# Two projections at a time, matmul by matmul: a two-layer macaron block in float32r on Trainium2

## The chip, the core and the metric

The kernel runs on one core of one Trainium2 chip. The metric is the device time of one execution in microseconds, as the median of several executions. One further execution was recorded by the hardware profiler; its rows are what the prediction reads. "PE" is TensorE's matmul pipe and "PEld" its weight loads, "DVE" is VectorE, "ACT" ScalarE, "POOL" GpSimd, "SP" the queue that issues all DMAs here.

## The reference, cut to what matters

```python
for l in range(2):                                            # x: 512 tokens x 1024
    h = 0.5 * swiglu(x, w_gate[l, 0], w_up[l, 0], w_down[l, 0])   # 1024 -> 2816 -> 1024
    x = layernorm(ALPHA * x + h, ...)
    u = x @ w_in[l]                                           # 1024 -> 1792
    u_conv, u_lru, q, k, v = split(u, [512, 1024, 1536, 1664])
    y = concat(conv_module(u_conv), recurrent(u_lru), sliding_window_attention(q, k, v))
    x = layernorm(ALPHA * x + y @ w_out[l], ...)
    h = 0.5 * swiglu(x, w_gate[l, 1], w_up[l, 1], w_down[l, 1])
    x = layernorm(ALPHA * x + h, ...)
```

`swiglu` is `(silu(x @ wg) * (x @ wu)) @ wd`. Everything is float32.

## The kernel before, in words

There are six phases: FFN, mixer, FFN for each of two layers (`phases`, line 749). The 512 tokens are the moving operand of the first products, held transposed: `xH` and `xL` are the high and low part of x as float32r, eight blocks of 128 features by 512 tokens each. A float32 product is made of three float32r products, low weights by `xH`, high weights by `xL`, high weights by `xH` (lines 312 to 314). `split` (line 116) makes the two parts of anything: a cast on ACT, then a subtraction on DVE.

**`proj`** (line 307) makes one output block: 128 columns of a weight matrix by all 512 tokens, accumulated in one PSUM bank over 8 blocks of features with three matmuls each, so 24 matmuls of 512 columns. The kernel before calls it for one bank at a time: in an FFN (line 359) first for the gate tile `pg`, then for the up tile `pu` (lines 386 and 387), 22 times per FFN; in the mixer (line 421) through `tile_of` (line 444), for one block of 128 of the 1792 input columns, when the program comes to need it. `proj_first` (line 295) makes the first four blocks of a phase in two halves of the tokens (256 columns each), because the last two token blocks of x are still being normalised: half 0 of block 0, the transposes of token block 2 (`to_xT(2)`), half 0 of blocks 1 and 2, `to_xT(3)`, half 0 of block 3, then half 1 of all four.

After the gate and up products `act` (line 370) applies Silu on ACT (line 372), multiplies on DVE (line 373) and splits. The down projection (`rowmm`, line 348) has the hidden units as stationary operand and 512 columns of weights as moving one; it cycles through eight banks, two per token block. The output projection of the mixer uses the same `rowmm` in `partial` (line 705) and `attn_out`.

In the mixer the order of the input blocks is `order` (line 436): recurrent input 4 and 5, keys 12, values 13, recurrent gate 6 and 7, queries 8, 9, 10, 11. `query(j)` (line 581) makes block 8+j and copies it out of its bank on ACT (line 582). Queries 0 and 1 are made ahead of attention; `query(2)` and `query(3)` stand in the attention loop:

```python
for u in range(U + 2):          # 8 units of 4 heads by 128 queries
    if u < U:
        scores(u)
    if u < 2:
        query(2 + u)
    ...
    if 0 <= u - 1 < U:
        transpose_p(u - 1)
```

`scores(u)` (line 642) issues four score matmuls on PE, then bias and row minimum on DVE (line 655), exponentials on ACT (line 662); `normalise` (line 667) scales by the reciprocal of the sum on ACT or DVE; `transpose_p` (line 679) turns the probabilities on PE, which ACT or DVE copies out (lines 689, 691), and `weighted` (line 694) multiplies by the values. One step runs on each of these for units u, u-1 and u-2 per turn of the loop.

The order of instructions on each engine is set by a scheduler that works from the order of the program and its own costs. Weights come through two buffers `raw` and 14 buffers of the pool `wpool` (seven pairs of high and low part); PSUM has eight banks, taken in turn by `bank()`. Some weight pairs lie in the pool `tpool` instead, whose tiles are 1030 floats wide and not 1024: the fourth pair of `wb` in the mixer's end (line 743) is one.

Of the kernel before, what the change touches and what calls it, by code (L numbers as in the profile page):

```python
# [22 lines left out]
KC = D // P  # L23
# [10 lines left out]
LOOK = 3  # L34
# [13 lines left out]
def tile_hymba(  # L48
# [38 lines left out]
    def nm(s):  # L87
        uid[0] += 1
        return f"{s}_{uid[0]}"

    def bank():
        return psum.tile([P, 512], F32, tag="ps", name=nm("ps"))
# [7 lines left out]
    def mm(o, a, b, start, stop):  # L100
        nc.tensor.matmul(o, a, b, start=start, stop=stop)  # L101
# [12 lines left out]
    xL = cpool.tile([P, KC, S], F32R, name="xL")  # L114

    def split(hi, lo, src):
        """src == hi + lo, both with the 12 significant bits of float32r."""
        nc.scalar.copy(hi, src)  # L118
        nc.vector.tensor_tensor(lo, src, hi.bitcast(F32), op=ALU.subtract)  # L119

    def to_xT(t):
        for hf in range(2):
            pt = bank()
            for c in range(4):
                k = hf * 4 + c
                nc.tensor.transpose(pt[:, c * P:(c + 1) * P], xs[:, t, k * P:(k + 1) * P], ident)  # L126
            sl = (slice(None), slice(hf * 4, hf * 4 + 4), slice(t * P, (t + 1) * P))
            split(xH[sl], xL[sl], pt.rearrange("p (c t) -> p c t", c=4))

# [1 line left out]
    chT = cpool.tile([P, 2, DEPTH * NCH], F32, name="chT")  # L131
    cpos = cpool.tile([P, 2, DEPTH], F32, name="cpos")
    cneg = cpool.tile([P, 2, DEPTH], F32, name="cneg")
# [65 lines left out]
    gates = {}  # L199
# [82 lines left out]
            norm_b(t, st, coef, last)  # L282

    class Start:
        """Weights of a phase's first products, loaded while the phase before ends."""

        def __init__(self, thunks):
            self.thunks = list(thunks)
# [2 lines left out]
        def load(self, n=1, pool=None):  # L291
            for _ in range(n):
                self.pairs.append(self.thunks.pop(0)(pool))

    def proj_first(items):
        def part(pb, w, lo, hi):
            proj([(pb, w)], ((lo, hi),))
        for n, (pb, w) in enumerate(items):
            if n == len(items) - 1:
                to_xT(3)  # L300
            part(pb, w, 0, 256)
            if n == 0:
                to_xT(2)
        for pb, w in items:
            part(pb, w, 256, 512)

    def proj(items, parts=((0, S),)):
        """items: (bank, weight pair); each part of the tokens is done for all of them in turn."""
        for lo, hi in parts:
            for pb, (wh, wl) in items:  # L310
                for k in range(KC):
                    mm(pb[:, lo:hi], wl[:, k, :], xH[:, k, lo:hi], k == 0, False)
                    mm(pb[:, lo:hi], wh[:, k, :], xL[:, k, lo:hi], False, False)
                    mm(pb[:, lo:hi], wh[:, k, :], xH[:, k, lo:hi], False, k == KC - 1)

    def fetch_raw(src):
# [18 lines left out]
    def load_cols(src, c, pool=None, raw=None):  # L335
        pair = load(cols(src, c), pool, raw)
        return [w.rearrange("p (k f) -> p k f", k=KC) for w in pair]
# [21 lines left out]
    def ffn(l, i, idx, start, nxt, last, hooks={}):  # L359
        wg, wu, wd = w_gate[l, i], w_up[l, i], w_down[l, i]  # L360
        for si, (f0, f1) in enumerate(SLABS):
            fin = si == len(SLABS) - 1
            hA = hpool.tile([P, 8, S], F32R, tag="hA", name=nm("hA"))
            hB = hpool.tile([P, 8, S], F32R, tag="hB", name=nm("hB"))
            hC = hpool.tile([P, HC], F32R, tag="hC", name=nm("hC"))[:, :6 * S].rearrange("p (a s) -> p a s", a=6)

            def hparts(n):
                return (hA[:, n, :], hB[:, n, :]) if n < 8 else (hC[:, n - 8, :], hC[:, n - 5, :])

            def act(f, pg, pu):  # L370
                sg = spool.tile([P, S], F32, tag="sg", bufs=2, name=nm("sg"))
                nc.scalar.activation(sg, pg, AF.Silu)  # L372
                nc.vector.tensor_tensor(sg, sg, pu, op=ALU.mult)  # L373
                split(*hparts(f - f0), sg)

            f = f0
            if f0 == 0:
                start.load(len(start.thunks))
                items = [(bank(), w) for w in start.pairs]
                proj_first(items)  # L380
                for j in range(2):
                    act(j, items[2 * j][0], items[2 * j + 1][0])
                f = 2
            while f < f1:
                pg, pu = bank(), bank()
                proj([(pg, load_cols(wg, f))])
                proj([(pu, load_cols(wu, f))])
                act(f, pg, pu)
                if f in hooks:
                    hooks[f]()  # L390
                f += 1
            ys = [[bank(), bank()] for _ in range(NT)]

            def hpair(f, t):
                return [h[:, t * P:(t + 1) * P] for h in hparts(f - f0)]

            flow = f1 - RESIDENT if fin else f1
            for f in range(f0, flow):
                w = load_rows(wd, f)
                for t in range(NT):  # L400
                    rowmm(ys[t], hpair(f, t), w, f == f0, f == f1 - 1)
            if not fin:
                for t in range(NT):
                    for hf, sl in enumerate(HS):
                        nc.vector.scalar_tensor_tensor(xs[:, t, sl], ys[t][hf], 0.5 / ALPHA, xs[:, t, sl],
                                                       op0=ALU.mult, op1=ALU.add)
                continue
            coef = ln_coef(idx)
            ws = [load_rows(wd, f) for f in range(flow, f1)]
            if nxt:  # L410
                nxt.load(3)
                nxt.load(1, tpool)

            def rows(t):
                for w, f in zip(ws, range(flow, f1)):
                    rowmm(ys[t], hpair(f, t), w, f == f0, f == f1 - 1)
                return ys[t]

            tail(rows, 0.5 / ALPHA, coef, last)

    def mixer(l, idx, start, nxt):
# [8 lines left out]
        wl = w_in[l]  # L430
# [5 lines left out]
        order = [4, 5, 12, 13, 6, 7, 8, 9, 10, 11]  # L436
        ahead = {}

        def fetch(n):
            for c in order[:n]:  # L440
                if c not in ahead:
                    ahead[c] = load_cols(wl, c)

        def tile_of(c):
            fetch(order.index(c) + LOOK)
            pb = bank()
            proj([(pb, ahead[c])])
            return pb

        # conv input and gate  # L450
        gate_in = [bank() for _ in range(4)]
        proj_first(list(zip(gate_in, start.pairs)))
        nc.gpsimd.memset(yc[:, :, 0:30], 0.0)
# [35 lines left out]
            if n == CONV_OUT_AT:  # L489
                conv_out(cv[0])  # L490

        # recurrent input
        xb = scratch()
        xbv = xb[:, :2 * (S + 3)].rearrange("p (c s) -> p c s", c=2)
        nc.gpsimd.memset(xbv[:, :, 0:3], 0.0)
# [8 lines left out]
                nc.vector.scalar_tensor_tensor(xc[:, c, :], xbv[:, c, k:k + S], ch(c, 34 + k), xc[:, c, :],  # L504
                                               op0=ALU.mult, op1=ALU.add)

        # keys and values
        pk = tile_of(12)
        for g in range(2):
            own = slice(64 * g, 64 * g + 64)  # L510
# [6 lines left out]
        nc.scalar.copy(vT[:, :S], pv)  # L517
        point()

        # recurrent gates  # L520
        rv = pair_of(wpool)
        iv = pair_of(wpool)
        qv = pair_of(wpool)
# [12 lines left out]
            for c in range(2):  # L536
                nc.scalar.activation(rv[:, c, :], nv[:, c, :], AF.Sqrt)

        # recurrent output gate
        gel = pair_of()  # L540
        for c in range(2):
            nc.scalar.activation(gel[:, c, :], tile_of(6 + c), AF.Gelu_apprx_tanh)
# [202 lines left out]
        nxt.load(4)  # L745
        tail(lambda b: partial(b, wb, (2, 3, 0, 1)), 1.0 / ALPHA, coef, False, lambda: attn_out(NT - 1, wo))

# [1 line left out]
    phases = []  # L749
    for l in range(DEPTH):  # L750
        phases += [(ffn, (l, 0, 3 * l), ffn_start(l, 0)), (mixer, (l, 3 * l + 1), mixer_start(l)),
# [1 line left out]
    with tc.manual_schedule():  # L753
        first = phases[0][2]
# [66 lines left out]
```

## Time and profile before

| what | value |
|---|---|
| median of 3 executions | 1845.03 us (1844.8, 1845.03, 1847.89) |
| profiled execution, first to last instruction (span) | 1850.2 us |
| its own device time | not listed apart from the span |
| PE busy | 1826.9 us (99%), 8530 matmul records |
| DVE / ACT / POOL busy | 828.8 us (45%) / 608.7 us (33%) / 35.1 us (2%) |
| DMA engines busy | 31.1%, 176.88 MB |
| chain that ended last | PE 92%, DVE 3%, ACT 2%, DMA 2% |

Matmul records are pipelined: one of 512 columns is listed with about 0.39 us, while the next one starts 0.23 us later. So PE's pace is read from starts, or from the number of records in a stretch, and not from the length of a record.

### The profile page before, as it was taken

The page shows a single profiled execution, that of the slowest core. Times are in us where ns is not written, and L with a number is a line of the kernel's source. Part 1 is how long each engine was busy: PE and PEld are TensorE (multiplying, and loading weights), DVE is VectorE, ACT ScalarE, POOL GpSimd, SP SyncE. Part 2 cuts the span into 40 slices and gives each one's busy share as a digit, 9 for nine tenths or more (in the row PEclk, how much of TensorE's full clock was granted, in tenths as well). Part 3 has the DMA queues.
Part 4 walks back from the last instruction along what each step waited for, and adds up shares of the span by engine and source line. Part 5 has one row for each costly group of instructions (what it writes and reads, how often), then busy time and mean ns, then how long its engine had stood idle before and what let it go on. Part 6 is the DMA issues. An engine that isn't in the chain of part 4 may idle for free.

```text
span 1850.2 us, 20960 instructions
## 1 busy us (share of the span) xinstructions
PE 1826.9 (99%) x8530; PEld 1490.9 (81%) x8530; DVE 828.8 (45%) x1281; ACT 608.7 (33%) x912; POOL 35.1 (2%) x76
## 2 busy tenths in 40 slices
PE   8999999999999999999999999999999999999998
PEld 7788888898678888888898888888976888888886
DVE  4342333269875332433363323333889833233324
ACT  4222222233954221222233212222458432222221
POOL 1000000000000000000000000000000100000000
PEclk9899999999999999999999999999999999999999
DMA  6433333222133323333333233323212332233321
GB/s 182 143 114 102 91 96 97 92 81 63 60 111 118 91 91 103 91 92 98 107 103 92 92 99 95 91 93 101 83 48 69 119 109 92 93 101 91 93 89 46
DMA packets 234248, 176.88 MB, mean 96 GB/s; under 512 B 6963, under 2 KB 217000, under 8 KB 234152
## 3 DMA queue, kind: packets, MB, share of 16 engines
q1 hardware_dynamic: 234152, 175.54, 31.1%
q8 instruction: 67, 1.10, 0.2%
q14 instruction: 29, 0.24, 0.0%
HBM read 171.33 MB, written 3.67 MB: 95 GB/s over the span
## 4 chain that ended last, share of the span: by engine, by line
PE 92%; DVE 3%; ACT 2%; DMA 2%; issue 0%; SPq 0%; POOL 0%; DVEq 0%; POOLq 0%; ACTq 0%
PE ps L101 91%; ACT t L662 1%; PE ps L126 1%; DVE wl L119 1%; DMA raw<-in_ffn_w_up_dram 1%; DMA raw<-in_ffn_w_gate_dram 1%; DMA xs<-in_x_dram 0%; ACT wh L118 0%; ACT t L675 0%; DMA raw<-in_w_out_dram 0%; DVE t L655 0%; DVE t L569 0%; DVE yL L119 0%; DVE t L254 0%; ACT junk L259 0%
## 5 line engine op out<-in xcount | busy, mean ns | idle before, releaser
L101 PE MATMUL ps<-xH,wl 128*128 128x512 f32 (+1 forms) x1824 | 683.9, 375 | 0.3 <-DVE wl L119 0.3
L101 PE MATMUL ps<-xL,wh 128*128 128x512 f32 (+1 forms) x1824 | 680.7, 373 | 1.0 <-DVE xL L119 1.0
L101 PE MATMUL ps<-xH,wh 128*128 128x512 f32 (+1 forms) x1824 | 680.4, 373 | 0.0
L119 DVE TENSOR_TENSOR wl<-raw,wh 128x1024 fp32r<-128x1024 f32 x308 | 376.1, 1223 | 630.2 <-ACT wh L118 629.5
L118 ACT CAST wh<-raw 128x1024 fp32r<-128x1024 f32 x308 | 323.3, 1052 | 1012.2 <-PE ps L101 953.3
L101 PEld LDWEIGHTS ps<-xH,wl 128*128 128x128 f32 x1824 | 345.2, 189 | 69.1 <-DVE t L236 1.1
L101 PEld LDWEIGHTS ps<-xL,wh 128*128 128x128 f32 x1824 | 345.3, 189 | 67.2 <-DVE xL L119 1.2
L101 PEld LDWEIGHTS ps<-xH,wh 128*128 128x128 f32 x1824 | 345.1, 189 | 66.2
L101 PE MATMUL ps<-wl,hA 128*128 128x512 f32 x512 | 199.4, 389 | 0.0
L101 PE MATMUL ps<-wh,hA 128*128 128x512 f32 x512 | 199.2, 389 | 0.0
L373 DVE TENSOR_TENSOR sg<-sg,ps 128x512 f32<-128x512 f32 x88 | 60.5, 687 | 306.0 <-PE ps L101 306.0
L101 PE MATMUL ps<-wh,hB 128*128 128x512 f32 x512 | 158.3, 390 | 0.0
L101 PE MATMUL ps<-wh,hC 128*128 128x512 f32 x384 | 121.5, 389 | 0.0
L101 PEld LDWEIGHTS ps<-wl,hA 128*128 128x128 f32 x512 | 96.1, 188 | 20.1
L101 PEld LDWEIGHTS ps<-wh,hA 128*128 128x128 f32 x512 | 96.1, 188 | 19.9
L101 PEld LDWEIGHTS ps<-wh,hB 128*128 128x128 f32 x512 | 95.7, 188 | 19.6
L101 PEld LDWEIGHTS ps<-wh,hC 128*128 128x128 f32 x384 | 72.1, 188 | 15.0
L463 DVE SCALAR_TENSOR_TENSOR t<-mix,chT,t 128x512 f32<-128x512 f32 x120 | 81.7, 742 | 0.2
L101 PE MATMUL ps<-wl,hC 128*128 128x512 f32 x192 | 74.7, 389 | 0.0
L372 ACT ACTIVATE sg<-ps 128x512 f32<-128x512 f32 x88 | 52.0, 591 | 4.3 <-PE ps L101 4.3
L259 ACT ACTIVATE junk<-t,nmean 128x1024 bf16<-128x1024 f32 x24 | 27.7, 1153 | 77.2 <-DVE nmean L257 77.2
L101 PE MATMUL ps<-wl,yH 128*128 128x512 f32 x128 | 50.7, 396 | 0.0
(134 smaller groups left out, 1015.9 us busy)
## 6 DMA issues: line engine op xcount, KB each, us to landing
raw<-in_ffn_w_gate_dram SPq DMA_DIRECT2D x88, 512.0 KB
raw<-in_ffn_w_up_dram SPq DMA_DIRECT2D x88, 512.0 KB
raw<-in_ffn_w_down_dram SPq DMA_DIRECT2D x88, 512.0 KB
raw<-in_w_in_dram SPq DMA_DIRECT2D x28, 512.0 KB
raw<-in_w_out_dram SPq DMA_DIRECT2D x16, 512.0 KB
t<-in_ln_g_dram SPq DMA_DIRECT2D x6, 512.0 KB
t<-in_ln_b_dram SPq DMA_DIRECT2D x6, 512.0 KB
xs<-in_x_dram SPq DMA_DIRECT2D x4, 512.0 KB
```

The source lines that it names most:

```text
L101: nc.tensor.matmul(o, a, b, start=start, stop=stop)
L118: nc.scalar.copy(hi, src)
L119: nc.vector.tensor_tensor(lo, src, hi.bitcast(F32), op=ALU.subtract)
L126: nc.tensor.transpose(pt[:, c * P:(c + 1) * P], xs[:, t, k * P:(k + 1) * P], ident)
L259: nc.scalar.activation(junk, z[:, :D], AF.Square, bias=nmean, accum_out=rs)
L372: nc.scalar.activation(sg, pg, AF.Silu)
L373: nc.vector.tensor_tensor(sg, sg, pu, op=ALU.mult)
L463: nc.vector.scalar_tensor_tensor(ca[:, c, :], yc[:, c, k:k + S], ch(c, k), ca[:, c, :], op0=ALU.mult, op1=ALU.add)
L662: nc.scalar.activation(s4[:, h, :nk], s4[:, h, :nk], AF.Exp, bias=nm_[:, h:h + 1], scale=-1.0, accum_out=sm[:, h:h + 1])
```

## The change

`proj` gets two items at a time and goes through them inside the loop over feature blocks: for each of the three kinds of product the matmul into the first bank is followed by the same one into the second. The gate and up tile of an FFN are such a pair, and so are blocks 0 and 1, and 2 and 3, of `proj_first`. In the mixer `tile_of` makes the block asked for and the next one of `order` together, so the pairs are 4 and 5, 12 and 13, 6 and 7, 8 and 9, 10 and 11. The rest of the diff drops comments.

```diff
     def proj_first(items):
-        def part(pb, w, lo, hi):
-            proj([(pb, w)], ((lo, hi),))
-        for n, (pb, w) in enumerate(items):
-            if n == len(items) - 1:
+        for n in range(0, len(items), 2):
+            if n == len(items) - 2:
                 to_xT(3)
-            part(pb, w, 0, 256)
+            proj(items[n:n + 2], ((0, 256),))
             if n == 0:
                 to_xT(2)
-        for pb, w in items:
-            part(pb, w, 256, 512)
+        for n in range(0, len(items), 2):
+            proj(items[n:n + 2], ((256, 512),))
...
         for lo, hi in parts:
-            for pb, (wh, wl) in items:
-                for k in range(KC):
+            for k in range(KC):
+                for pb, (wh, wl) in items:
                     mm(pb[:, lo:hi], wl[:, k, :], xH[:, k, lo:hi], k == 0, False)
+                for pb, (wh, wl) in items:
                     mm(pb[:, lo:hi], wh[:, k, :], xL[:, k, lo:hi], False, False)
+                for pb, (wh, wl) in items:
                     mm(pb[:, lo:hi], wh[:, k, :], xH[:, k, lo:hi], False, k == KC - 1)
...
                 pg, pu = bank(), bank()
-                proj([(pg, load_cols(wg, f))])
-                proj([(pu, load_cols(wu, f))])
+                proj([(pg, load_cols(wg, f)), (pu, load_cols(wu, f))])
                 act(f, pg, pu)
...
+        made = {}
+
         def tile_of(c):
-            fetch(order.index(c) + LOOK)
-            pb = bank()
-            proj([(pb, ahead[c])])
-            return pb
+            if c not in made:
+                n = order.index(c)
+                fetch(n + 1 + LOOK)
+                two = order[n:n + 2]
+                for d in two:
+                    made[d] = bank()
+                proj([(made[d], ahead[d]) for d in two])
+            return made[c]
```

Two places of the scheduled order matter below. The first is ACT in the first mixer, around the scores of units 0 and 1. `t_3126` and `t_3127` are the query tiles (first and second pair), so a copy into `t_3127` marks the end of a product of query block 10 or 11; `t_3216` is unit 0's score tile, `t_3287` (before) and `t_3312` (after) unit 1's; the wide casts are weights. From `tile_of` on, lines of the changed kernel stand five further down (582 is 587). Before:

```order
L664 ACTIVATE es_3228<-es_3228 128x4
L118 CAST wh_3431<-raw_3429 128x1024
L675 ACTIVATE t_3216<-t_3216,ri_3281 128x128
L582 ACTIVATE t_3127<-ps_3236 128x512
L675 ACTIVATE t_3216<-t_3216,ri_3281 128x128 x3
L118 CAST wh_3480<-raw_3478 128x1024
L662 ACTIVATE t_3287,sm_3301<-t_3287,nm_3288 128x256 x4
L664 ACTIVATE es_3299<-es_3299 128x4
L118 CAST wh_3542<-raw_3540 128x1024
L552 ACTIVATE tw_3048<-tw_3048,cneg 128x512
L554 ACTIVATE tw_3048<-tw_3048,half 128x512 x2
L582 ACTIVATE t_3127<-ps_3307 128x512
```

And now:

```order
L667 ACTIVATE t_3216,sm_3230<-t_3216,nm_3217 128x128 x4
L669 ACTIVATE es_3228<-es_3228 128x4
L118 CAST wh_3373<-raw_3371 128x1024
L680 ACTIVATE t_3216<-t_3216,ri_3306 128x128 x4
L118 CAST wh_3431<-raw_3429 128x1024
L557 ACTIVATE tw_3048<-tw_3048,cneg 128x512 x2
L587 ACTIVATE t_3127<-ps_3236 128x512
L587 ACTIVATE t_3127<-ps_3237 128x512
L559 ACTIVATE tw_3048<-tw_3048,half 128x512
L667 ACTIVATE t_3312,sm_3326<-t_3312,nm_3313 128x256 x4
L669 ACTIVATE es_3324<-es_3324 128x4
```

Unit 1's exponentials stood between the copies of query blocks 10 and 11, and now stand behind both. The weight cast that stood directly ahead of them is gone from that place, and one of the two steps at line 559 (554 before) stands there instead.

The second place is DVE at the same point; `t_3287`, `t_3312` and the casts are as above, `wl` is the low part of a weight tile. Before:

```order
L119 TENSOR_TENSOR wl_3432<-raw_3429,wh_3431 128x1024
L655 ISA t_3287,nm_3288<-ps_3289,nbias,nsink 128x256
...
L119 TENSOR_TENSOR wl_3481<-raw_3478,wh_3480 128x1024
L659 TENSOR_TENSOR es_3299<-nm_3288,sink 128x4
L670 TENSOR_TENSOR sm_3301<-sm_3301,es_3299 128x4
L672 RECIPROCAL ri_3345<-sm_3301 128x4
L677 TENSOR_SCALAR t_3287<-t_3287,ri_3345 128x256 x4
L119 TENSOR_TENSOR wl_3543<-raw_3540,wh_3542 128x1024
L556 SCALAR_TENSOR_TENSOR tw_3049<-tw_3049,tw_3048 128x512 x2
```

And now:

```order
L119 TENSOR_TENSOR wl_3374<-raw_3371,wh_3373 128x1024
L119 TENSOR_TENSOR wl_3432<-raw_3429,wh_3431 128x1024
L660 ISA t_3312,nm_3313<-ps_3314,nbias,nsink 128x256
...
L561 SCALAR_TENSOR_TENSOR tw_3049<-tw_3049,tw_3048 128x512
L664 TENSOR_TENSOR es_3324<-nm_3313,sink 128x4
L565 SCALAR_TENSOR_TENSOR tw_3048<-tw_3049,tw_3048 128x512
L660 ISA t_3351,nm_3352<-ps_3353,nbias,nsink 128x128
```

Two weight subtractions now stand ahead of unit 1's scores, and none directly behind them. On PE the products themselves alternate: of the matmuls of `proj` that directly follow another one, 5241 went into the same bank as the one before them, and 32 do now (all in the first pair of the first phase, where the scheduler lets the gate run ahead of the up weights).

## Rows read from the trace of the kernel before

**Rows 1.** The page's part 1 (busy) and part 4 (chain), whole execution.

```profile
PE 1826.9 (99%) x8530; PEld 1490.9 (81%) x8530; DVE 828.8 (45%) x1281; ACT 608.7 (33%) x912; POOL 35.1 (2%) x76
...
PE 92%; DVE 3%; ACT 2%; DMA 2%; issue 0%; SPq 0%; POOL 0%; DVEq 0%; POOLq 0%; ACTq 0%
```

**Rows 2.** Windows, line 101: down, then gate and up (us, records, clock, DMA).

```profile
160.00:200.00 40.00, 40.00 (x178) 1.00 0.34 102
240.00:300.00 60.00, 60.00 (x258) 1.00 0.32 93
```

**Rows 3.** Instruction groups by shape, whole execution: one of three kinds of product.

```profile
L101 PE MATMUL ps<-xH,wl 128*128 128x512 f32 x1440 | 574.0, 399 | 0.0
```

**Rows 4.** Timeline of PE (start, length): end of an up product, then down.

```profile
151.12 0.40 PE L101 MATMUL ps<-xL,wh 128*128 128x512 f32 x1
151.35 0.39 PE L101 MATMUL ps<-xH,wh 128*128 128x512 f32 x1
151.59 0.63 PE L101 MATMUL ps<-wh,hB 128*128 128x512 f32 x2
152.05 0.39 PE L101 MATMUL ps<-wl,hA 128*128 128x512 f32 x1
```

**Rows 5.** Timeline of PE, end of a block of the output projection.

```profile
545.72 0.62 PE L101 MATMUL ps<-wh,yL 128*128 128x512 f32 x2
...
547.08 0.63 PE L101 MATMUL ps<-wh,yL 128*128 128x512 f32 x2
...
548.25 0.40 PE L101 MATMUL ps<-wh,yH 128*128 128x512 f32 x1
```

**Rows 6.** Chain in order of time (start, us, what), first mixer.

```profile
464.99 12.01 PE ps L101 x54
...
477.01 0.60 ACT t L582
...
478.48 0.94 ACT wh L118
...
483.08 1.14 DVE wl L119
484.22 1.20 DVE tw L556 x2
...
486.51 0.61 DVE tw L560
...
493.72 1.13 PE ps L101 x2
```

**Rows 7.** The same view, second mixer.

```profile
1369.91 17.31 PE ps L101 x70
...
1403.96 1.13 PE ps L101 x2
```

**Rows 8.** Timeline, first mixer, all engines.

```profile
477.98 0.51 PE L101 MATMUL ps<-xH,wl 128*128 128x512 f32 x1
...
482.96 1.33 ACT L554 ACTIVATE tw<-tw,half 128x512 f32<-128x512 f32 x2
...
483.71 0.60 PE L687 MATMUL ps<-ident,t 128*128 128x128 f32 x4
```

**Rows 9.** Timeline, first phase, all engines.

```profile
21.71 1.23 DVE L119 TENSOR_TENSOR wl<-raw,wh 128x1024 fp32r<-128x1024 f32 x1 [0.94 <-ACT wh L118]
...
39.87 0.40 PE L101 MATMUL ps<-xH,wl 128*128 128x512 f32 x1
```

**Rows 10.** Timeline, from the first FFN to the first mixer.

```profile
396.80 0.28 PE L101 MATMUL ps<-xH,wl 128*128 128x256 f32 x1
...
399.65 1.04 PE L126 MATMUL ps<-ident,xs 128*128 128x128 f32 x8
...
402.06 1.42 DVE L270 SCALAR_TENSOR_TENSOR xs<-xs,rs,t 128x512 f32<-128x512 f32 x2 [0.83 <-POOL rs L261]
```

**Rows 11.** Windows, all engines: the stretch of the bias products (PE, PEld, DVE, ACT, POOL).

```profile
77.00:87.00 10.00, 10.00 (x21) 6.16 (x20) 3.47 (x7) 0.00 (x0) 0.00 (x0) 0.50 0.69 232
```

## The prediction

> **What bounds the kernel now.** I read the page's busy times and its chain first: PE is busy 99% of a span of 1850.2 us, and the chain that ended last runs over PE for 92% of it [rows 1]. So time can come from two places only: from PE's pace while it is busy, or from stretches where the chain leaves PE. The next views take one each.
>
> For the pace I count records in windows without any stall. In a stretch of gate and up products a window of 60 us touches 258 matmuls of 0.40 us each, so the spacing is (60 + 0.40) / 258 = 0.2341 us; in the down projection it is (40 + 0.39) / 178 = 0.2269 us [rows 2]. Both stretches have the full clock, 1.00. There are 3 x 1440 = 4320 products of the slower kind with 512 columns [rows 3], which is 1011 us, more than half of the span.
>
> For the stretches away from PE I read the chain in order of time in the mixers. It is on PE until unit 1's scores are done, at 477.01. From there to 493.72 it is on ACT and DVE, through copies, exponentials, weight casts and recurrence steps, and PE is not on it at all [rows 6]. The second mixer shows the same: PE until 1369.91 + 17.31 = 1387.22, and again from 1403.96 [rows 7]. In each of these 16.7 us PE is busy all the same, because the product of query block 11 lies in them, from 477.98 to 483.71 [rows 8]. That product is the cover of unit 1's softmax.
>
> **The change part by part.**
>
> *Alternating banks.* The number of matmuls, weight loads, columns and DMAs stays the same. What could change is the spacing of 0.2341 us, if the second of two matmuls into one bank waited for the first. The down projection is the faster one and cycles through banks, so it looks like an argument for that. It is not one: two of the six steps in each round of `rowmm` stay in one bank, and its mean is 0.2269 us all the same. The direct test is a place where the bank changes. At the end of an up product, the last matmul starts at 151.35, and the next, into another bank, at 151.59, 0.24 us later; the two before it are 0.23 us apart [rows 4]. A waiting bank would have given its time back there. The other test is a change of pace without any change of the bank pattern. In a block of the output projection the six matmuls from 545.72 to 547.08 take 1.36 us, 0.227 each; the last six come from the fourth weight pair of `wb`, the one in the pool with tiles of 1030 floats, and five spacings of those take 548.25 - 547.08 = 1.17 us, 0.234 each [rows 5]. Same line, same banks in the same order, another place of the moving operand in SBUF. The two paces are just those of the two projections. I take it that the pace belongs to the moving operand's tile, `xH` and `xL` here, which the change does not move. Price: 0. The ends: 4320 x (0.2341 - 0.2269) = 31 us gained if the bank were the cause after all; on the other side, the weights that were loaded twice in a row (`wh` for two products) now alternate. The down projection has repeated and changing stationary operands in one stretch at one spacing [rows 2, 4], so I see no loss either; 1% of the pace would be 10 us.
>
> The Trainium skill, TensorE: Matmul & The Clock Gate, section on the back-to-back issue gap, gives N / 2.4 + 2.5 ns for isolated matmuls, 216 ns for 512 columns. Rows 2 show no stretch that fast. If the whole excess over that figure were the bank's, an estimate from the page is 4320 x 18 ns = 78 us gained; by the rows it is at most 31 us, and I count none.
>
> *The mixer.* Query block 11 moves ahead of unit 1's scores, because it is now made with block 10. Its 24 x 0.2341 = 5.62 us leave the stretch in which the chain is on ACT and DVE and are added to the stretch in which it is on PE. So unit 1's softmax starts 5.62 us later and has that much less cover. If ACT and DVE did the same work after it, all of it would be lost. Part comes back, because both have time now under the longer pair of products: by the scheduled order the weight cast (0.94 us) and the weight subtraction (1.14 us) that lie in the chain [rows 6] move ahead of unit 1's scores, while one of the two steps at line 554, half of 1.33 us less their overlap, about 0.6 us [rows 8], comes between. 5.62 - 0.94 - 1.14 + 0.6 = 4.1 us. The ends: all 5.62 us; or, with the recurrence steps in the chain moved out as well (1.20 and 0.61 us), 5.62 - 0.94 - 1.14 - 1.20 - 0.61 = 1.7 us. Two mixers: **8.2 us lost**, between 3.4 and 11.2. What is late next is the value product of unit 0, whose probabilities ACT copies out only behind unit 1's exponentials, and then the transposes of unit 1, behind DVE's scaling.
>
> The pairs 4 and 5, 12 and 13, 6 and 7 deliver their first block 5.6 us later and the second when it came before. Nothing on PE waits for them soon, and ACT and DVE are off the chain until 477.01 [rows 6]: 0. Query 9 now precedes the gate matmuls, which come later and wait less: 0.
>
> *The first phase.* The third product of `proj_first` needed only the second gate tile, now it needs the up tile with it, whose low part is ready at 21.71 + 1.23 = 22.94 [rows 9]. From there 144 of the 256-column products remain. One of these takes (399.65 - 396.80) / 24 = 0.119 us [rows 10], so they end at 22.94 + 17.1 = 40.1, against 39.87 now [rows 9]: 0.2 us lost, up to 2 if the wait lets the clock fall.
>
> *The five later phase starts.* `to_xT(3)` comes earlier. Token block 3 is ready at 402.06 + 1.42 = 403.48. `to_xT(2)` will start at 399.65 + 24 x 0.119 = 402.5 and takes 1.04, so `to_xT(3)` comes at 403.5 [rows 10]. It just fits: 0. If it slipped, each 0.1 us of lateness would show five times. The splits that follow have the 48 products of pair 2 and 3 as cover, 5.7 us, against 24 before.
>
> *The FFN.* Silu of a gate tile had the up product as cover and now starts with both done. Only the last tile of a half FFN can be felt: its banks go to the fourth token block of the down projection, 18 x 0.2269 = 4.1 us later [rows 2]. A cast that stands ahead, Silu, the multiplication and a subtraction all fit in: 0. Weights are freed two pairs at a time, with five pairs still loaded, 28 us of products: 0. The SP queue keeps its DMAs; pairs of raw tiles change places, and POOL's order is the same.
>
> **Sum.** 8.2 + 0.2 = 8.4 us. On the profiled execution that is 1850.2 + 8.4 = 1858.6 us of span. The three timed executions lie lower than this one, which holds one more stretch of low clock; on their median it is 1845.0 + 8.4 = **1853.4 us**. Its own range, from the ends of the mixer and the first phase: 3.4 to 13.2 us, 1848.4 to 1858.2 us. About 0.2%, 3.7 us, is what a measurement of this kernel tells from no change.
>
> **The rivals.**
>
> *A. The bank was the bound.* All 4320 products fall to the pace of the down projection, 31 us, and the mixers cost 8.4: 1845.0 - 31 + 8.4 = 1822 us. For it: the faster projection is the one that alternates. Against it: the spacing at the bank's change, and the two paces at one bank pattern [rows 4, 5]. Half of it would still be faster, 1838 us. It decides from 2 ns per product: below that the mixers eat it.
>
> *B. The softmax is covered after all.* ACT and DVE get so far ahead under the longer pair that the lost cover does not count: 1845 to 1848 us. For it: DVE is 45% and ACT 33% busy [rows 1]. Against it: what they can do ahead does not depend on unit 1's scores, and the softmax itself does.
>
> *C. More than the cover is lost.* A longer idle of PE lets its clock fall. In the stretch of the bias products the granted clock was 0.50, 1.2 instead of 2.4 GHz, and 21 matmuls took 10 us [rows 11]; the engine had run products of 33 rows with short waits before that. A 512-column product then takes 512 / 1.2 GHz = 0.43 us, so 20 of them cost 4 us more. One such fall in each mixer gives 1853.4 + 8 = 1861 us. That the bias products lose theirs is as likely; it would give 4 us back.
>
> *D. Cycling banks makes PE idle briefly between groups and the clock swing.* The down projection cycles through eight banks at 1.00 [rows 2], so I give this almost nothing; at 0.43 us for every tenth product it would be 432 x 0.19 = 82 us, 1935 us. The Trainium skill, TensorE: Matmul & The Clock Gate, second failure mode (queue cycling through banks), reports such swings and speaks against this change; by that rule the clock of the FFN stretches would change, and rows 2 do not agree.
>
> *E. The alternation does not happen.* The scheduler could undo it; the order shows it in 5418 of 5450 places. No chance given.
>
> **How the numbers follow.** Forecast 62%, A 13% (half of it partial), B 14%, C 9%, D 2%. Faster than 1841.3: A and a trace of C's other side, 0.14. Within 0.2%: B, and the forecast's lower end, 0.17. Slower: 0.69. The range of 8 in 10 leaves out A and the top of C and D: 1843 to 1861 us.
>
> **What would show it.** The gate and up window again holds 258 records in 60 us; 266 would mean A. Around unit 1's scores PE should wait once for some 2 to 3 us at the value product of unit 0 with ACT as releaser, and shorter after that, in both mixers. In the first phase the 512-column products should start near 40.1. The prediction is wrong if the mixers' stretches are no longer than before, or if the spacing moves by over 1 ns.

## The result and the profile after

The changed kernel takes 1859.14 us (median of 4 executions, 1858.51 to 1861.12) against 1845.51 us (1844.8 to 1847.89): 13.6 us slower, ratio 1.0075 with an interval of 1.006 to 1.0089. The forecast was 1853.4 us, 8.4 us slower. Its own range ended at 1858.2 us, 13.2 us slower; the range of 8 in 10, with the rivals, at 1861. So the result lies above what the sum allowed, inside the wider range, and nearer to rival C's 1861 than to the forecast. Executions of one kernel differ by several microseconds, the long ones at a lower mean granted clock: with block 9 ahead of the gates, below, 1856.2 us at 0.996 and 1865.2 us at 0.991.

The page's part 1 and part 4 of the changed kernel, beside [rows 1]:

```profile
PE 1826.0 (98%) x8530; PEld 1489.8 (80%) x8530; DVE 820.1 (44%) x1281; ACT 601.8 (32%) x912; POOL 37.4 (2%) x76
...
PE 93%; DVE 3%; ACT 2%; DMA 1%; issue 0%; SPq 0%; POOL 0%; DVEq 0%; POOLq 0%; ACTq 0%
```

On the level of the page nothing has happened. The profiled execution took 1858.5 us for a span of 1856.7, so 1.8 us lie around a span. By that the profile of before, with its span of 1850.2, was some 6 us longer than its median execution: it held low clock in the bias stretch [rows 11] and once more at the end of the first mixer, behind its attention. The two spans are 6.5 us apart, the medians 13.6, and the profiles have to be compared stretch by stretch.

The pace, in the same windows of line 101 as [rows 2] (us, PE records, clock, DMA):

```profile
160.00:200.00 40.00, 40.00 (x178) 1.00 0.31 92
240.00:300.00 60.00, 60.00 (x258) 1.00 0.30 88
```

258 records again in 60 us, at full clock: alternating the banks gave nothing and cost nothing. From the start of the FFN behind the first mixer to the first 512-column product of the second mixer's blocks the profiles show 766.28 us, before 766.36.

What is left is the mixers. The timeline of PE in the changed kernel has the marks (start, length, what; in brackets the idle time ahead and what ended it):

```profile
417.81 0.63 PE L101 MATMUL ps<-xH,wl 128*128 128x512 f32 x2
...
483.55 1.12 PE L101 MATMUL ps<-t,mix 128*128 128x512 f32 x2 [2.33 <-ACT t L696]
...
521.87 2.54 PE L101 MATMUL ps<-t,mix 128*128 128x512 f32 x4 [2.48 <-ACT t L696]
...
533.84 1.02 PE L101 MATMUL ps<-wh,yL 128*128 128x512 f32 x2
...
1396.88 1.17 PE L101 MATMUL ps<-t,mix 128*128 128x512 f32 x1 [2.32 <-ACT t L696]
...
1436.63 0.70 PE L101 MATMUL ps<-t,mix 128*128 128x512 f32 x1 [2.48 <-ACT t L696]
```

The first row starts the mixer's 512-column products and the fourth the last 120 products of its output projection: 533.84 - 417.81 = 116.03 us. Before it was 531.51 - 421.14 = 110.37:

```profile
421.14 0.39 PE L101 MATMUL ps<-xH,wl 128*128 128x512 f32 x1
...
531.51 0.79 PE L101 MATMUL ps<-wh,yL 128*128 128x512 f32 x1
```

In the second mixer it is 117.48 against 110.41. The waits at 483.55 and 1396.88, for ACT's copy of unit 0's probabilities, are those of the prediction ("once for some 2 to 3 us"). Those at 521.87 and 1436.63 are as long, and no step had them.

The waits had a consequence that stood only among the rivals. Windows of PE (us, busy, clock, DMA):

```profile
523.20:526.50 3.30, 3.30 (x8) 0.50 0.07 21
1397.00:1400.30 3.30, 3.30 (x6) 0.50 0.00 0
1438.00:1441.30 3.30, 3.30 (x8) 0.50 0.06 16
```

After three of the four long waits the clock stood at 0.50 for about 3.4 us; after the one at 483.55 it did not. In the kernel before the clock was full in both attention stretches.

The first phase: the third product waits for the low part of the up weights, as foreseen, and the 512-column products start at 39.68 (forecast 40.1, before 39.87 [rows 9]).

```profile
22.64 0.35 PE L101 MATMUL ps<-xH,wl 128*128 128x256 f32 x1 [2.62 <-DVE wl L119]
...
39.68 0.63 PE L101 MATMUL ps<-xH,wl 128*128 128x512 f32 x2
```

### The profile page after: what moved, and what is told of

It is laid out like the page before. It is cut to its first block, busy times and chain, and to the rows that moved or that the text cites. A ratio compares the mean times of both kernels' runs of the same rounds, so it can differ in the third digit from the quotient of the medians.

```text
span 1856.7 us, 20890 instructions
## 1 busy us (share of the span) xinstructions
PE 1826.0 (98%) x8530; PEld 1489.8 (80%) x8530; DVE 820.1 (44%) x1281; ACT 601.8 (32%) x912; POOL 37.4 (2%) x76
## 4 chain that ended last, share of the span: by engine, by line
PE 93%; DVE 3%; ACT 2%; DMA 1%; issue 0%; SPq 0%; POOL 0%; DVEq 0%; POOLq 0%; ACTq 0%
PE ps L101 92%; PE ps L126 1%; ACT t L667 1%; DVE wl L119 1%; DMA raw<-in_ffn_w_up_dram 1%; DVE t L660 0%; DMA xs<-in_x_dram 0%; DVE yL L119 0%; DVE xs L721 0%; ACT t L696 0%; PE ps L692 0%; DVE t L574 0%; ACT wh L118 0%; DVE t L254 0%; ACT junk L259 0%
## 5 line engine op out<-in xcount | busy, mean ns | idle before, releaser
L101 PE MATMUL ps<-xH,wl 128*128 128x512 f32 (+1 forms) x1824 | 534.4, 373 | 2.6 <-DVE wl L119 2.6
L101 PE MATMUL ps<-xL,wh 128*128 128x512 f32 (+1 forms) x1824 | 533.4, 373 | 0.1
L101 PE MATMUL ps<-xH,wh 128*128 128x512 f32 (+1 forms) x1824 | 532.6, 373 | 0.0
L101 PEld LDWEIGHTS ps<-xH,wl 128*128 128x128 f32 x1824 | 331.2, 189 | 69.3 <-issue 2.8
L101 PEld LDWEIGHTS ps<-xL,wh 128*128 128x128 f32 x1824 | 331.8, 189 | 66.7 <-DVE xL L119 0.4
L101 PEld LDWEIGHTS ps<-xH,wh 128*128 128x128 f32 x1824 | 331.8, 189 | 66.3
```

## The experiments

All times are medians beside runs of the kernel before on the same chip (1845.7 to 1845.9 us). "Mixer" is the stretch measured above, first and second mixer of the profiled execution, with the time at half clock in it in brackets where there was any.

| kernel | us | ratio (interval) | mixer 1 | mixer 2 |
|---|---|---|---|---|
| before | 1845.5 | | 110.37 | 110.41 |
| the change | 1859.1 | 1.0075 (1.006 to 1.0089) | 116.03 (3.4) | 117.48 (6.8) |
| gate and up pairs alone | 1846.0 | 1.0001 (0.9992 to 1.0009) | 110.48 | 110.52 |
| mixer pairs alone | 1858.4 | 1.0062 (1.0047 to 1.0077) | 117.75 (10.2) | 117.77 (6.8) |
| 10 and 11 apart | 1861.4 | 1.0086 (1.0072 to 1.01) | 116.66 (3.4) | 116.66 (3.4) |
| 8 and 9 apart | 1853.8 | 1.0042 (1.0026 to 1.0059) | 113.61 (6.8) | 113.58 (6.8) |
| 8 to 11 apart | 1849.2 | 1.002 (1.001 to 1.0029) | 110.48 | 110.41 |
| all pairs, gates first | 1859.5 | 1.0072 (1.0051 to 1.0094) | 114.73 (3.4) | 114.93 (3.4) |
| before, block 9 ahead of the gates | 1861.3 | 1.008 (1.0052 to 1.0107) | 120.12 (13.7) | 116.49 (3.4) |

### Which part costs: FFN or mixer

Gate and up pairs alone (the mixer and `proj_first` as before):

```diff
-                proj([(pg, load_cols(wg, f))])
-                proj([(pu, load_cols(wu, f))])
+                proj([(pg, load_cols(wg, f)), (pu, load_cols(wu, f))])
```

> Gate and up alternate as in the change, but the mixer makes its blocks one at a time and the first four blocks of a phase are made one at a time, as before. 4224 of the matmuls of 512 columns alternate. My theory (the alternation costs and gives nothing, the whole loss is query block 11 moved ahead of unit 1's scores): 1845.5 us, ratio 0.998 to 1.002, the spacing in a stretch of gate and up products 234 ns as before, and around unit 1's scores of the mixers the waits of the kernel before. Rival 1 (alternating banks and weights cost a little at every matmul, or at every tile's end where Silu now starts later): the FFN holds 4224 of the 4704 changed matmuls, so most of the 13.6 us would be here, 1855 us or more. Rival 2 (alternation does gain and the mixer loses more than the whole): under 1842 us.

1846.02 us, ratio 1.0001. Its gate and up window:

```profile
240.00:300.00 60.00, 60.00 (x257) 1.00 0.31 89
```

The mixer's pairs alone (the new `tile_of`, the rest as before):

> Only the mixer makes its blocks in pairs; gate and up, and the first four blocks of a phase, one at a time as before. My theory: the whole loss is here, 1857 to 1860 us, ratio 1.006 to 1.0085, with the value product of unit 0 waiting some 2.5 us and a second wait of some 2.6 us later in attention, in both mixers. Rival 1 (a cost at every alternating matmul): 480 matmuls of the mixers alternate of 4704, so under 1850 us.

1858.37 us. Rival A fell, and so did any cost of the alternation: the first kernel, with 3840 alternating matmuls of 512 columns (the expectation's 4224 counts the first four blocks of each FFN in), moves the time by less than the interval; the second, with 480, by 12.6 us.

### Which pair of the mixer

Query blocks 10 and 11 made one at a time, all else as in the change:

```diff
-                fetch(n + 1 + LOOK)
-                two = order[n:n + 2]
+                two = order[n:n + 2] if n < 8 else [c]
+                fetch(n + len(two) - 1 + LOOK)
```

> The change, but query blocks 10 and 11 are made one at a time, so that block 11 comes again behind unit 1's scores; every other pair stays (gate and up, 4 and 5, 12 and 13, 6 and 7, 8 and 9, and the first four blocks). My theory (the cover of unit 1's softmax is what was lost): 1845 to 1848 us, ratio 1.000 to 1.002, and PE waits under 0.5 us at the value product of unit 0 as before. Rival (the other pairs of the mixer, by shifting when their blocks are copied and the recurrence starts, lose a good part of it): 1850 to 1855 us, with the second wait, 2.6 us in the change, still there.

1861.43 us: not a microsecond came back, and my theory fell. Unit 0's value product hardly waits now, but PE waits elsewhere, and one wait of 2.40 us is the one that no step of the prediction had:

```profile
498.12 1.12 PE L101 MATMUL ps<-t,mix 128*128 128x512 f32 x2 [1.56 <-ACT t L696]
...
522.92 1.63 PE L101 MATMUL ps<-t,mix 128*128 128x512 f32 x2 [2.40 <-ACT t L696]
```

The chain of this kernel in order of time says where its loss begins. PE leaves the chain at 463.62, at the end of blocks 8 and 9, and is back on it at 498.12 only. That is 45.4 us into the mixer, which starts at 418.27 here; in [rows 6] PE holds the chain until 477.01, 55.9 us into it:

```profile
459.86 3.76 PE ps L101 x16
...
463.64 1.08 ACT t L587 x2
...
464.74 1.28 ACT L535
...
498.12 7.02 PE ps L101 x26
```

Line 535 is the first sigmoid of the recurrence's gates, and the 1.28 us ahead of it an activation-table load. From 463.62 to 498.12 the chain is on ACT for 26.5 us and on DVE for 6.4. So the new theory was: the gates come 5.6 us later, because block 9 was moved ahead of them, and ACT starts later on a load that it cannot make up. In the change itself, though, PE is on the chain until 479.99, 62.2 us into the mixer, so there the late gates are not what ends last ahead of unit 1's scores:

```profile
454.95 25.03 PE ps L101 x108
```

Three runs were made on the theory.

Blocks 8 and 9 apart, 10 and 11 paired:

> The change, but query blocks 8 and 9 are made one at a time (10 and 11 and all others in pairs). So the matmuls of the recurrence's gates stand between blocks 8 and 9 again, as before. Theory of the prediction (the loss is block 11 moved ahead of unit 1's scores): 1851 to 1859 us. Theory since query blocks 10 and 11 apart changed nothing (the loss is that the recurrence's gates come 5.6 us later on PE, so that their exponentials, steps and copies on ACT and DVE run into the attention units): 1845 to 1849 us, ratio up to 1.002.

All four apart, the other pairs kept:

> The change, but query blocks 8 to 11 are all made one at a time; the pairs left are gate and up, 4 and 5, 12 and 13, 6 and 7, and the first four blocks of a phase. Both theories of the loss (query 11's cover, the later gates of the recurrence): 1845 to 1847 us, ratio 0.999 to 1.001. Rival (the pairs 4 and 5, 12 and 13, 6 and 7, costed at nothing, cost something): 1850 us or more.

All pairs as in the change, the gates ahead of blocks 8 and 9:

```diff
-        query(0)
         gate_block()
+        query(0)
```

> The change with one line of the program moved: the recurrence's gate matmuls stand ahead of the pair of query blocks 8 and 9 and not behind it, so they start some 11 us earlier in the mixer than in the change, and 5.6 us earlier than in the kernel before. All pairs stay. Theory of the later gates: the loss goes, 1843 to 1848 us. Theory of query 11's cover: it stays, 1853 us or more. If both count, between the two.

With 8 and 9 apart: 1853.8 us, 3.2 us in each mixer. That is inside what the prediction gave to block 11 (1.7 to 5.6), and over what the new theory said of it; unit 0's value product waits for unit 1's exponentials as foreseen:

```profile
483.84 1.13 PE L101 MATMUL ps<-t,mix 128*128 128x512 f32 x2 [2.11 <-ACT t L696]
```

With all four apart the mixers are back at 110.4 to 110.5; the 3 us over the kernel before are not in them. Its profile reaches the first mixer 5.3 us later than that of gate and up pairs alone (422.50 against 417.20), and 3.5 of them are there when the first phase's 512-column products start. With the gates first the mixers still take 114.7 and 114.9, and 1859.5 us fit only what was expected of block 11's cover, 1853 or more: the new theory alone is not enough either. Each of the two moves costs, and block 11 costs whether the gates are early or not.

### The place of block 9 without any pairing

The last step is to make the move and nothing else. The kernel before, with block 9 made ahead of the gates (`tile_of` also keeps what it has made, which is left out here):

```diff
         query(0)
+        tile_of(9)
         gate_block()
```

> The kernel before with one thing changed: query block 9 is made ahead of the recurrence's gate matmuls and not behind them. No two blocks are interleaved anywhere, and blocks 10 and 11 stand where they stood. Theory (the pairing of 8 and 9 costs because it puts block 9 ahead of the gate matmuls, by which ACT's work starts 5.6 us later): as with 8 and 9 paired alone, 6 us for each mixer, 1856 to 1860 us, ratio 1.006 to 1.008, and PE waits some 1.7 us at a value product and 2.6 us at a later one. Rival (the interleaving of the two products itself, or the copy of block 8 that comes later, costs): 1845 to 1849 us.

1861.32 us, just above the 1856 to 1860 expected: with no two products interleaved anywhere, the whole loss of the pair is there, 116.49 us in the second mixer against 116.66 with 8 and 9 paired, and the wait at the later value product too:

```profile
524.73 1.00 PE L101 MATMUL ps<-t,mix 128*128 128x512 f32 x1 [2.41 <-ACT t L695]
```

So the place of block 9 costs. What passes the delay on is less clear. A row of the kernel before that could have warned is one of ACT's timeline, with a window of ACT behind it (us, busy, clock, DMA):

```profile
461.13 0.60 ACT L582 ACTIVATE t<-ps 128x512 f32<-128x512 f32 x1 [4.49 <-PE ps L101]
461.74 1.28 ACT L530 ACT_TABLE_LOAD   x1
```

```profile
461.00:477.00 16.00, 15.32 (x27) 1.00 0.24 74
```

ACT idles 4.49 us until block 8 and the gates are there, and from then on it is busy in 15.32 of 16 us. It is not on the chain there, but it has little slack. In the change it idles twice as long and starts 45.4 us into the mixer instead of 40.0:

```profile
463.19 1.09 ACT L587 ACTIVATE t<-ps 128x512 f32<-128x512 f32 x2 [9.62 <-PE ps L101]
```

That ACT's queue is what passes the delay on is argued from this, and not shown for every part. In the kernel with block 9 ahead and nothing paired PE holds the chain of the first mixer until 473.23, 56.5 us into it, about as long as before:

```profile
455.00 18.23 PE ps L101 x79
```

And ahead of the later wait of the change, from 496.09 to 521.87, the chain lies on DVE for 18.5 us and on ACT for 5.6. On it are the recurrence's two scans (line 574), apart from each other, and at its end ACT's copy:

```profile
502.22 1.14 DVE t L574
...
508.77 1.14 DVE t L574
...
521.23 0.59 ACT t L696
```

Before, the scans stand together (line 569):

```profile
502.06 2.25 DVE t L569 x2
```

There the second scan ends 83.2 us into the mixer. In the four kernels with block 9 ahead of the gates (the change, mixer pairs alone, 10 and 11 apart, and this one) it ends at 92.1 to 96.0, and each of their mixers has the later wait of 2.4 to 2.5 us; in the others of the table it ends at 64.0 to 85.5, and none has that wait. This points to the recurrence's steps on DVE as a second path of the delay; no run moved these steps alone.

### Why the projections are slower than the down projection

The spacing of 0.2341 us stayed as it was under every order of the banks. The prediction put it down to the tile of the moving operand. The pools place `xH` at byte 33504 of a partition, `xL` 16384 behind it, and all weight tiles of the main pool and the hidden activations at 64 past a multiple of 512. The kernel before with `mhalf` allocated behind `xL`, so that the big tiles start 32 bytes earlier:

> The kernel before with one small tile allocated behind xL and not ahead of xs, so that xs, xH and xL start 32 bytes earlier in a partition (at 17088, 33472 and 49856, multiples of 64) and nothing else moves; the work and its order are the same. My theory (the pace of the projections belongs to the place of the moving operand): the spacing in a gate and up stretch falls from 234 to 227 ns, the pace of the down projection, whose moving tiles start at multiples of 64; 4320 x 7.4 ns = 32 us, and if the 256-column products gain in the same ratio, 1152 x 3.6 ns = 4 us: 1809 to 1815 us, ratio 0.981 to 0.984. Rival (the pace belongs to something else that the two projections differ in, banks or the kind of operand): 1845.5 us and 234 ns as before.

1840.41 us, ratio 0.9972 (0.996 to 0.9984). Something moved, but not to 227: 259 records in the window, spacings of 229 and 238 ns in turn, 233.3 in the mean.

```profile
240.00:300.00 60.00, 60.00 (x259) 1.00 0.30 90
```

Next the big tiles behind all small parameter tiles (`chT`, `cpos`, `cneg`, `sink`, `nsink`), at 34368 and 50752, 64 past a multiple of 512 like the weights:

> The kernel before with the big tiles xs, xH and xL allocated behind the small parameter tiles, so that xH and xL start at bytes 34368 and 50752 of a partition; like the weight tiles of the main pool (104000, then every 4096) they are then 1600 past a multiple of 2048. Work and order are the same. Moving them by 32 bytes took a gate and up matmul from 234.3 to 232.4 to 233.3 ns, which is neither my 227 nor no change. Theory now (the pace goes by where the moving operand starts relative to the stationary one, modulo some hundred bytes): 227 ns, as in the down projection, which has both 1600 past a multiple of 2048; 4320 x 7.5 ns, so about 1811 us, ratio 0.980 to 0.983. Rival (the place is a side effect, and the projections are slower for another reason): 231 ns or more, 1835 us or more.

**1817.07 us**, ratio 0.9841 (0.9826 to 0.9856): 28.8 us faster than the kernel before, by the place of three tiles, though some 6 us short of the 1811 us expected. The projections now run at the pace of the down projection:

```profile
160.00:200.00 40.00, 40.00 (x179) 1.00 0.34 103
240.00:300.00 60.00, 60.00 (x267) 1.00 0.32 97
```

Start of the moving operand, or its distance from the stationary one? An unused tile ahead of the weight pools moves weights and activations by 32 bytes and leaves `xH` and `xL`:

```diff
     junk = cpool.tile([P, D], BF16, name="junk")
+    fill = cpool.tile([P, 4], F32, name="fill")
+    nc.vector.memset(fill, 0.0)
```

> The kernel before with an unused tile of 16 bytes behind the constants, which moves every later pool, the weight tiles and the hidden activations among them, by 32 bytes; xs, xH and xL stay. Weight tiles then start at 104032, and moving and stationary operand of the down projection keep their distance. Two readings of what the placing runs showed. Reading 1 (the pace goes by the start of the moving operand alone): the down projection falls to the 234 ns that the output projection showed for moving tiles 32 past a multiple of 64: 2112 of its matmuls and most of the 384 of the output projection, some 2400 x 7.5 ns = 18 us, 1860 to 1867 us, ratio 1.008 to 1.012. Reading 2 (it goes by the distance between moving and stationary operand): the down projection keeps 226.7 ns, and the projections, whose distance changes by 32, move instead.

1840.9 us, ratio 0.9971 (0.9959 to 0.9982). The down projection keeps its pace though its moving tiles now start elsewhere, and the projections go to 233.3 ns, just as when `xH` itself was moved by 32 bytes the other way:

```profile
160.00:200.00 40.00, 40.00 (x178) 1.00 0.31 92
240.00:300.00 60.00, 60.00 (x259) 1.00 0.32 97
```

So it is the distance. Modulo 512 it is 160 bytes in the kernel before (234.3 ns), 128 in the two kernels moved by 32 bytes (233.3), and 0 in the fast one and in every down projection (226.7).

Two runs asked what else goes with the better place. Gate and up pairs on it:

> xs, xH and xL placed as in the run that took 1817 us, and gate and up alternating as in the change; the mixer's blocks and the first four of a phase one at a time. Theory (banks cost nothing at either pace): 226.7 ns in the gate and up stretch and 1816 to 1819 us, as without the pairs. Rival (with the distance of the operands out of the way the bank becomes the bound, and alternating pays now): under 226 ns, 1812 us or less.

1816.26 us (1814.72 to 1818.35), 266 records in the window: no gain from alternating at the faster pace either. And the gates ahead of block 8, nothing paired:

> The kernel before with xs, xH and xL at 1600 past a multiple of 2048, as in the run that took 1817 us, and with the recurrence's gate matmuls ahead of query block 8 and not between 8 and 9; nothing is paired. Theory (ACT is the bound from the gate matmuls on, so where they stand on PE sets the end of attention): they come 5.5 us earlier, and both mixers end earlier, by up to 5.5 us each: 1806 to 1814 us. Rival (something else ends last when the gates come earlier, the scores or DVE, as the kernel with gates first and all pairs suggests, which regained only 1.2 to 2.7 us of a mixer): 1814 to 1820 us.

1819.74 us (1816.14 to 1820.62): no gain, a miss of my theory. Its first mixer takes 110.10 us, where the better place alone takes 108.81. Earlier gates did not help, while later ones cost; so in the kernel before the gates seem just early enough, and the next bound behind them was not looked for.

## Why the prediction was right, and where not

**Right: the alternation.** Price 0, by the spacing at a bank's change and by two paces at one bank pattern [rows 4, 5]. Four kernels with and without pairs, at two paces, agree. The reading that the pace belongs to the operands' place was right in kind, and half right in its subject: the stationary operand's place counts as well. Rival D did not come: the FFN windows stand at 1.00. The Trainium skill, TensorE: Matmul & The Clock Gate, section on a second failure mode, tells of clock swings where banks are cycled; the 4320 alternating products bring none here, and the low stretches are the ones behind the bias products, which the kernel before has too, behind PE's waits in attention, and at the program's end. The 216 ns of its section on the issue gap are not reached either: the fastest stretch of any run has (60 + 0.39) / 267 = 226.2 ns by this coarse count, 226.7 from start to start.

**Too small, and wrong in part: the mixer.** It was to lose 8.2 us, between 3.4 and 11.2; it lost 5.7 + 7.1 = 12.7. The step that failed is the sentence "Query 9 now precedes the gate matmuls, which come later and wait less: 0." Alone, in a kernel without any pairing, this move costs 6.1 us in the second mixer (116.49 - 110.41). I had tested it by the chain, on which ACT is not before 477.01 [rows 6], and not by how full ACT is ahead of that, nor by when DVE gets the recurrence's steps. Being off the chain was read as having slack.

The step on block 11 held in its place and its sign: in the change the chain leaves PE at unit 1's scores, and unit 0's value product waits 2.3 us. Its size came out by luck in part: 4.1 us taken, 3.2 measured alone, and most of that is not waiting (see the clock, below). The two moves do not add: 6.2 and 3.2 apart, 5.7 and 7.1 together, and with block 11 back in its place nothing is regained as long as the gates are late. Why was not tested.

**Undersized: the clock.** Rival C had it at 9%. How much of the loss is waits and how much slower work can be read from windows of PE over the mixers (us, busy and records, clock, DMA): before, in the change, and with 8 and 9 apart.

```profile
421.14:531.51 110.37, 108.32 (x490) 1.00 0.21 64
1331.36:1441.77 110.41, 108.32 (x491) 1.00 0.20 63
```

```profile
417.81:533.84 116.03, 109.81 (x490) 0.99 0.21 65
1331.14:1448.62 117.48, 111.40 (x491) 0.97 0.20 64
```

```profile
417.96:531.57 113.61, 111.10 (x491) 0.97 0.21 67
1329.15:1442.73 113.58, 111.11 (x490) 0.97 0.20 66
```

Length less busy time is 2.05 and 2.09 us of idle before, 6.22 and 6.08 in the change. So 8.2 of its 12.7 us are waits. The other 4.6 us are longer busy time for the same products, with 10.2 us at half clock in it, 0.45 us per us; that the clock is all of it is an estimate, since the order of the products differs too. That the waits come to the forecast 8.2 us is luck: of the 4.2 us more in the first mixer some 2.5 stand around units 0 and 1, where the forecast had 4.1, and the rest behind them, where it had none.

With 8 and 9 apart, so with block 11's move alone, PE idles 2.51 and 2.47 us, only 0.4 to 0.5 us more than before: the wait of 2.11 us stands in the place of several smaller ones. The other 2.8 of the 3.2 us are busy time, with 6.8 us at half clock in it. So the lost cover by itself cost little waiting, and by this reading the fall of the clock, rival C's, made most of the loss there.

The two mixers of one program are no safe measure of the price. Three kernels give 0.35 to 0.43 us per us at half clock (117.48 with 6.8 against 116.03 with 3.4 in the change), but mixer pairs alone give none (117.75 with 10.2, 117.77 with 6.8).

Rival C rested on a row that it misread. There were no "short waits" before the fall of the clock in the bias stretch: by the records PE was busy throughout until 76.7, with products of 33 rows 0.32 us apart from 74.1 on (us, busy and records, clock, DMA). So that row does not bear out that an idle PE loses its clock; the falls behind the long waits of the mixers fit it, though not every such wait brought one.

```profile
62.00:76.70 14.70, 14.70 (x60) 1.00 0.25 73
```

**The first phase.** The time was right (39.68 against 40.1), the difference was not. Five profiles with paired first blocks start the 512-column products at 39.7 to 41.1, 40.3 in the mean; nine with single ones at 37.6 to 39.9, 38.4 in the mean. So the term is 1.9 us and not 0.2, inside its "up to 2": the profile of before that I subtracted from happened to be the latest of the nine. The two latest of the five, 40.8 and 41.1, hold 3.4 us at half clock behind the wait for the up weights, as foreseen; the other three are at 39.9 in the mean. 1849.15 against 1846.02 us, of the kernel with 8 to 11 apart and the one with gate and up pairs alone, points the same way.

**The sum.** 12.7 + 1.9 = 14.6, measured 13.6. Phase starts, FFN and the pairs 4 and 5, 12 and 13, 6 and 7 were costed at 0, and are: 24.45 against 24.34 us from a mixer's first block to its 512-column products, 766.28 against 766.36 for two FFNs, 110.4 to 110.5 us for mixers that keep just these pairs.

## What to carry to other kernels

Before a product is moved ahead of another, look at what starts when the other one ends, and at all that hangs on it later. Here ACT was off the chain but busy in 96% of the stretch behind the gates, and the recurrence's steps on DVE hung on it; the gates came 5.6 us later, and the mixer ended 6.1 us later, with 3.4 us at half clock in it. A step costed at nothing wants a row that shows the slack, and a difference to the profile of before wants more than one profile of before. Interleaving for the sake of banks is worth a test with two paces and one bank pattern; here the pace was in the addresses, and reordering allocations gave 28.8 us.

## What was not expected of the hardware

The pace of a 128x512 matmul depended on the distance, modulo 512 bytes, between its moving and its stationary tile in SBUF: 226.7 ns at 0, 233.3 at 128, 234.3 at 160, at full clock and whatever the bank. Whether other distances are as good as 0, and what the modulus is exactly, is open. The 256-column products did not gain: from a mixer's first 256-column product to its first 512-column one it is 24.66 us at the better place and 24.34 in the kernel before.

A wait of PE of over 2 us in attention was followed by a stretch at half clock in most places and not in all (in the change in three of four). Two stretches of 10.2 us came without one: with the gates first at the better place behind waits of 1.17 and 0.43 us, and with block 9 ahead of the gates behind waits of 0.86 and 0.54 us. In the other mixer of the first of these kernels the same waits were followed by none.
